# A hybrid attention / delta-net / PEER block: weights, U and V laid out anew, split weights kept in DRAM for the second half, and 448 gathered rows ahead of the dense pass

## The chip, the core and the metric

The kernel runs on one core of a Trainium2 chip. Its engines are TensorE (PE, matmuls into PSUM), VectorE (DVE), ScalarE (ACT), GpSimd (POOL) and SyncE (SP); 16 DMA engines move data between DRAM and the on-chip SBUF. SP issues the ordinary loads and stores of this kernel, POOL the indirect ones that gather rows by index. The metric is the device time of one execution in microseconds (us). The kernel before was run three times besides its profiled execution.

## The reference

One decoder block over 1024 tokens of width 1024, all float32: two token mixers in parallel, a gated merge, and a PEER feed-forward layer of 16,384 single-neuron experts. Cut to what matters here:

```python
h = rms_norm(x, mix_norm_w)
proj = h @ w_in            # 3x1024 stick-breaking q,k,v; 4x1024 delta net q,k,v,z; 16 b,a; 2x1024 gates
o_sb = stick_breaking_attention(q, k, v)                   # 8 heads of 128
o_gdn = gated_delta_rule_chunked(gq, gk, gv, g, beta)      # 8 heads of 128, then norm and silu(z)
merged = sigmoid(gate_sb) * (o_sb @ w_branch_sb) + sigmoid(gate_gdn) * (o_gdn @ w_branch_gdn)
x = x + merged @ w_out
h2 = rms_norm(x, ffn_norm_w)
q = h2 @ w_q                                               # 8 heads x 2 x 128
v1, i1 = top_k(q_1 @ keys1.T, 16); v2, i2 = top_k(q_2 @ keys2.T, 16)
vals, c = top_k(v1[..., :, None] + v2[..., None, :], 16)   # 16 of 256 pairs per head
expert = i1[c // 16] * 128 + i2[c % 16]; gate = softmax(vals)
# each token: 8 heads x 16 experts, with multiplicity
x = x + sum_over_experts(gate * gelu(h2 . peer_u[expert]) * peer_v[expert])
```

## The kernel before

**Numbers.** A float32 operand goes into TensorE as two rounded parts, hi and lo: `split` (L58) casts on ACT (L62) and subtracts on DVE (L63). `mm3` (L68) then makes three matmuls, hi·hi, hi·lo and lo·hi (L71 to L73).

**Stages.** The 1024 tokens are done in two halves of 512 (`half(0)`, `half(1)`). Each half runs stick-breaking attention (four pairs of heads), the gated delta net (four pairs), `gate_logits`, `merge`, `out_proj`, `ffn_norm` and `route`. Every weight comes through `load_w` (L87) in blocks of 256 columns: 12 for the attention, 16 for the delta net, 8 for the logits, 8 for the two branch matrices, 4 for `w_out` and 8 for `peer_w_q`, so 56 for each half, and one of 16 columns. A block is loaded on SP as two raw pieces of 512 KB (L93) and split in four pieces of 128x512; the pools `wp` and `wraw` hold two blocks and two raw pieces. The second half loads and splits the same weights again. A block serves 48 matmuls with 512 columns.

**The expert layer** is done in two ways. The token blocks 0, 1, 4 and 5 (128 tokens each) gather their rows: 128 experts a token, for U and for V, so 4 × 256 = 1024 indirect loads of 128 rows (512 KB, POOL, L1016), each followed by one DVE instruction over 128x1024 (L1019 for U, L1021 for V). The token blocks 2, 3, 6 and 7 go densely over all 128 blocks of 128 experts: `dense` (L856). For these, `gate_table` (L808) builds the full table of gates, 128 x 128 experts for each token, from one-hot matmuls, and stores it to DRAM (`g_d`, L854, 16 stores of 2 MB); `gates` loads it back, four expert blocks at a time (`d_g`, L906).

In the dense loop one expert block takes: `prep`, which loads 128 rows of U, transposes them with eight TensorE transposes (L877) into PSUM and splits them in two pieces; `scores`, 24 matmuls (L891, L893) and a Gelu (L895); `weigh`, the product with the gates (L922), the cast (L926) and the rest of the split (L913); `values`, which loads and splits rows of V; and 24 value matmuls into four PSUM accumulators (`pz1` and `pc`, two banks each), which are added to `d_acc` every eight blocks (L974). Scores run ahead of the weighing: seven are made inside the gate table's stage, spread over its four token blocks, and six weighings before the loop.

**Order.** A scheduler orders each engine's instructions by priority, in which `later(n)` puts work back. The gathered rows have the lowest priority, and each is tied behind an anchor: `gather(phase)` stands at the program's own steps and lets `PACE[phase]` rows go per step, behind the last DVE instruction issued there (L1028 to L1058). They begin with the second half; with the numbers of before, 353 of the 1024 rows stand ahead of the first weighing in DVE's order and the others in the dense loop. Four row buffers serve them, six within the dense loop. An engine executes its instructions in order, so a row whose data is late holds the DVE work behind it.

## Time and profile before

| | |
|---|---|
| runs | 3888.91, 3900.24, 3903.44 us; median 3900.24 |
| the profiled execution: time, span | 3908.46 us, 3906.7 us |
| busy: PE, DVE, ACT, POOL | 3674.3, 3089.5, 1753.0, 1298.8 us |
| moved by DMA | 939.72 MB, 241 GB/s over the span |
| the gathers' queue / the other loads and stores | 536.94 MB / 399.22 MB |
| mean granted PE clock | 0.971 |

The span is the profiled execution from its first to its last instruction. The profile gives each engine's busy time by source line and tile, what ended each wait, and how busy the 16 DMA engines were. The stages differ in what limits them, so the totals are read together with a table by stretch of the span. Line numbers are those of the kernel before.

### The profile page before, as it was taken

Reading aid. Unit: us, or ns where it says so; the run is one execution under the profiler, and the core shown is the slowest. Engines: PE = TensorE matmul, PEld = TensorE weight load, DVE = VectorE, ACT = ScalarE, POOL = GpSimd, SP = SyncE. Lnnn points to the kernel's source line nnn. Section 1 sums busy time; section 2 is a strip of 40 time slices with the busy share of each in tenths; the row PEclk is TensorE's granted clock in tenths of the full one; section 3 lists DMA queues with packets and bytes.
Section 4 is the critical chain, followed back from the end, with each engine's and each line's share of the span. In section 5 each row is a group of like instructions: output and inputs, shape, how many; then the busy total and the mean of one; then the engine's idle time right before and its main releaser. Section 6 shows DMA issues by size and latency. Waiting matters only on the chain. (4 is left out here: it accounts for less than half of the span.)

```text
span 3906.7 us, 55712 instructions
## 1 busy us (share of the span) xinstructions
PE 3674.3 (94%) x19976; PEld 3077.4 (79%) x19976; DVE 3089.5 (79%) x6330; ACT 1753.0 (45%) x3986; POOL 1298.8 (33%) x1034
## 2 busy tenths in 40 slices
PE   8999999999999999998877995899999999999997
PEld 7878888787777688886666884788888888888886
DVE  4345554349988988888789998899898899899898
ACT  6755555333777655543322994222222222222321
POOL 0000000000144322233341113655566555566555
PEclk9999999999999999999888998999999999999998
DMA  5221114552387766578884568899999999999998
GB/s 141 86 83 50 55 49 127 167 190 88 103 275 263 240 196 190 161 229 290 309 283 147 214 230 305 307 353 363 334 362 355 332 354 352 335 360 351 351 347 297
DMA packets 448230, 939.72 MB, mean 241 GB/s; under 512 B 44113, under 2 KB 239697, under 8 KB 445521
## 3 DMA queue, kind: packets, MB, share of 16 engines
q0 software_dynamic: 147456, 536.94, 39.1%
q1 hardware_dynamic: 300496, 399.22, 30.5%
q8 instruction: 157, 2.57, 0.3%
q14 instruction: 121, 0.98, 0.1%
HBM read 865.27 MB, written 70.25 MB: 239 GB/s over the span
## 5 line engine op out<-in xcount | busy, mean ns | idle before, releaser
L1016 POOL DMA_INDIRECT gb_row<-peer_u,expert x512 | 670.0, 1309 | 1879.1 <-DVE expert L796 1013.5
L1016 POOL DMA_INDIRECT gb_row<-peer_v,expert x512 | 627.6, 1226 | 714.9 <-DVE gb_h L1021 464.1
L1021 DVE SCALAR_TENSOR_TENSOR gb_h<-gb_row,gb_act,gb_h 128x1024 f32<-128x1024 f32 x512 | 656.1, 1281 | 60.6 <-DMA gb_row<-peer_v,expert 33.1
L1019 DVE SCALAR_TENSOR_TENSOR gb_row<-gb_row,gb_h 128x1024 f32<-128x1024 f32 x512 | 613.0, 1219 | 97.4 <-DMA gb_row<-peer_u,expert 77.6
L891 PE MATMUL mm<-hf,ut 128*128 128x512 f32 x2048 | 514.2, 398 | 0.0
L891 PEld LDWEIGHTS mm<-hf,ut 128*128 128x128 f32 x2048 | 376.1, 188 | 70.7
L63 DVE TENSOR_TENSOR w_lo<-w_raw,w_hi 128x512 fp32r<-128x512 f32 (+1 forms) x456 | 298.4, 676 | 166.7 <-ACT w_hi L62 128.5
L62 ACT CAST w_hi<-w_raw 128x512 fp32r<-128x512 f32 (+1 forms) x456 | 262.9, 615 | 275.6 <-PE mm L72 127.5
L71 PE MATMUL mm<-h,w_hi 128*128 128x512 f32 (+1 forms) x784 | 322.4, 411 | 4.0 <-ACT pj L587 4.0
L73 PE MATMUL mm<-h,w_lo 128*128 128x512 f32 (+1 forms) x784 | 319.9, 408 | 0.0
L72 PE MATMUL mm<-h,w_hi 128*128 128x512 f32 (+1 forms) x784 | 319.2, 407 | 0.0
L71 PE MATMUL mm<-w_hi,h 128*128 128x256 f32 x1024 | 301.3, 295 | 9.2 <-DVE x L636 4.7
L73 PE MATMUL mm<-w_hi,h 128*128 128x256 f32 x1024 | 294.6, 289 | 5.7 <-DVE h L63 5.7
L926 ACT CAST d_a<-u_act 128x512 fp32r<-128x512 f32 x128 | 79.4, 621 | 484.7 <-DVE u_act L922 483.9
L72 PE MATMUL mm<-w_lo,h 128*128 128x256 f32 x1024 | 296.0, 289 | 0.7 <-DVE w_lo L63 0.7
L893 PE MATMUL mm<-hf,ut 128*128 128x512 f32 x1024 | 260.3, 391 | 0.0
L895 ACT ACTIVATE u_act<-mm 128x512 f32<-128x512 f32 x128 | 77.0, 601 | 390.2 <-PE mm L893 376.5
L71 PE MATMUL pz<-d_v,d_a 128*128 128x512 f32 x512 | 201.6, 394 | 45.1 <-ACT d_a L926 30.8
L62 ACT CAST d_v<-v_raw 128x1024 fp32r<-128x1024 f32 x128 | 134.3, 1050 | 208.0 <-PE pc L73 175.9
L893 PEld LDWEIGHTS mm<-hf,ut 128*128 128x128 f32 x1024 | 192.3, 188 | 38.9
L71 PEld LDWEIGHTS mm<-w_hi,h 128*128 128x128 f32 x1024 | 200.6, 196 | 17.3 <-DVE x L636 5.2
L73 PEld LDWEIGHTS mm<-w_hi,h 128*128 128x128 f32 x1024 | 200.7, 196 | 7.8 <-DVE h L63 5.9
(332 smaller groups left out, 8632.4 us busy)
## 6 DMA issues: line engine op xcount, KB each, us to landing
w_raw<-w_in SPq DMA_DIRECT2D x144, 512.0 KB
u_raw<-peer_u SPq DMA_DIRECT2D x128, 512.0 KB
v_raw<-peer_v SPq DMA_DIRECT2D x128, 512.0 KB
g_d<-gt_stg SPq DMA_DIRECT2D x16, 2048.0 KB
d_g<-g_d SPq DMA_DIRECT2D x31, 1024.0 KB
w_raw<-peer_w_q SPq DMA_DIRECT2D x32, 512.0 KB
gl<-pj SPq DMA_DIRECT2D x32, 256.0 KB
th<-gl SPq DMA_DIRECT2D x32, 256.0 KB
```

The source lines that it names most:

```text
L62: nc.scalar.copy(hi, src)
L63: nc.vector.tensor_tensor(lo, src, hi.bitcast(F32), op=OP.subtract)
L71: mm(out, l[0], r[0], start=first, stop=False)
L72: mm(out, l[0], r[1], start=False, stop=False)
L73: mm(out, l[1], r[0], start=False, stop=last)
L891: mm(ps, ut[0][:, k], hx[a][:, k, x0:], start=k + a == 0, stop=False)
L893: mm(ps, ut[1][:, k], hx[0][:, k, x0:], start=False, stop=k == KD - 1)
L895: nc.scalar.activation(act, ps, AF.Gelu)
L926: nc.scalar.copy(hi, act)
L1016: nc.gpsimd.indirect_dma_start(out=r, out_offset=None, in_=self.i["peer_u" if p < n else "peer_v"][0], in_offset=bass.IndirectOffsetOnAxis ...
L1019: i = nc.vector.scalar_tensor_tensor(r, r, 1.0, h2, op0=OP.mult, op1=OP.mult, accum_out=act[:, q:q + 1])
L1021: i = nc.vector.scalar_tensor_tensor(acc, r, act[:, q:q + 1], acc, op0=OP.mult, op1=OP.add)
```

## The change

1. The host lays the inputs out anew before the launch: all projection weights as blocks of 256 columns, contiguous for each partition; the 16 columns of b and a apart (`w_ba`); the keys transposed (so `keys_T` with its 16 transposes goes); U transposed within each block of 128 experts (`u_t`); V by pairs of expert blocks and halves of the width (`v_t`). The raw copies of U and V stay for the gathers.
2. `load_w` keeps hi and lo of each block in DRAM when it is first used (two stores of 1 MB, in the first half). In the second half it loads hi and lo (two loads of 1 MB) straight into their places and splits nothing.
3. `prep` loads U already transposed into a pool of its own (two buffers) and splits it in one piece; its transposes go.
4. The gate table in DRAM has another order: a store of 2 MB now writes runs of 512 bytes, and a load reads 8 KB for each partition in one run (before 16 KB and 512 bytes).
5. Of the seven scores ahead, three are made within the gate table's stage and four behind its last matmul.
6. The four value accumulators rotate over six PSUM banks (`bank`).
7. `PACE` lets 448 rows go ahead of the dense pass and 4.5 a block within it.

```diff
-PACE = dict(sb=2.2, gdn=1.5, logits=2.5, merge=2.5, out=0.5, route=0, table=0.1, dense=5.25)
+PACE = dict(sb=2.4, gdn=2.4, logits=3, merge=2.5, out=0.5, route=0, table=0.1, dense=4.5)
...
-    def load_w(self, src, c0, n=CB):
-        hi = self.wp.tile([P, KD, n], F32R, name="w_hi")
-        lo = self.wp.tile([P, KD, n], F32R, name="w_lo")
+    def load_w(self, src, c0):
+        hi = self.wp.tile([P, KD, CB], F32R, name="w_hi")
+        lo = self.wp.tile([P, KD, CB], F32R, name="w_lo")
+        key = (src.tensor.name, c0)
+        if key in self.w_d:
+            for d, t in zip(self.w_d[key], (hi, lo)):
+                self.nc.sync.dma_start(t.bitcast(F32), d)
+            return hi, lo
         for k0 in range(0, KD, 4):
-            raw = self.wraw.tile([P, 4, n], F32, name="w_raw")
-            self.nc.sync.dma_start(raw, src[k0 * P:(k0 + 4) * P, c0:c0 + n].rearrange("(k p) n -> p k n", p=P))
+            raw = self.wraw.tile([P, 4, CB], F32, name="w_raw")
+            self.nc.sync.dma_start(raw, src[c0 // CB][:, k0:k0 + 4])
             for k in range(k0, k0 + 4, 2):
                 self.split(hi[:, k:k + 2], lo[:, k:k + 2], raw[:, k - k0:k - k0 + 2])
+        self.w_d[key] = [self.dr.tile([P, KD, CB], F32, name=f"wd{len(self.w_d)}_{a}") for a in range(2)]
+        for d, t in zip(self.w_d[key], (hi, lo)):
+            self.nc.sync.dma_start(d, t.bitcast(F32))
         return hi, lo
...
-                        mm(pg[:, u - u0], o2[:, u], o1[:, u], start=True, stop=True)
+                        self.last_gate = mm(pg[:, u - u0], o2[:, u], o1[:, u], start=True, stop=True)
...
-            nc.sync.dma_start(self.g_d[(n * P + c * GT) // GT], stg)
+            nc.sync.dma_start(self.g_d[:, :, (n * P + c * GT) // GT].rearrange("g p q t -> p g (q t)"),
+                              stg.rearrange("p (g q) t -> p g (q t)", q=GQ))
...
+            ur = pool(name="ur", bufs=2)
             def prep(e1):
-                raw = up.tile([P, D], F32, name="u_raw")
-                nc.sync.dma_start(raw, U[e1 * P:(e1 + 1) * P, :])
+                raw = ur.tile([P, KD, P], F32, name="u_raw")
+                nc.sync.dma_start(raw, U[e1])
                 ut = [up.tile([P, KD, P], F32R, name=f"ut{a}") for a in range(2)]
-                for k0 in range(0, KD, 4):
-                    ps = self.pz.tile([P, 4, P], F32, name="pz0")
-                    for k in range(4):
-                        nc.tensor.transpose(ps[:, k], raw[:, (k0 + k) * P:(k0 + k + 1) * P], self.ident)
-                    self.split(ut[0][:, k0:k0 + 4], ut[1][:, k0:k0 + 4], ps)
+                self.split(ut[0], ut[1], raw)
                 return ut
...
-                    nc.sync.dma_start(gts[-1][:, c:c + nc_],
-                                      self.g_d[c:c + nc_, :, e1:e1 + GQ, :].rearrange("c p q t -> p c q t"))
+                    nc.sync.dma_start(gts[-1][:, c:c + nc_], self.g_d[e1 // GQ][:, c:c + nc_])
...
+            def bank():
+                self.turn = (self.turn + 1) % 3
+                return (self.pc if self.turn == 2 else self.pz).tile([P, 512], F32, name=("pz0", "pz1", "pc")[self.turn])
...
-                nc.sync.dma_start(raw, V[e1 * P:(e1 + 2) * P, dh * 512:dh * 512 + 512].rearrange("(q p) d -> p q d", p=P))
+                nc.sync.dma_start(raw, V[e1 // 2, dh])
...
                     self.gate_table(n, blk, gt)
-                    for e1 in range(PRE * n // nb, PRE * (n + 1) // nb):
+                    if n < nb - 1:
+                        scores()
+                with self.tc.issue_after(self.last_gate.ins):
+                    while len(acts) < PRE:
                         scores()
...
                 if q == 0:
-                    ps = [self.pc.tile([P, 512], F32, name="pc") if n % 2 else self.pz.tile([P, 512], F32, name="pz1")
-                          for n in range(nb)]
+                    ps = [bank() for n in range(nb)]
...
-        b.g_d = dr.tile([len(b.dense_blks) * P // GT, P, P, GT], F32, name="g_d")
+        b.g_d = dr.tile([P // GQ, P, len(b.dense_blks) * P // GT, GQ, GT], F32, name="g_d")
```

Three places show how the instructions stand. The first is PE's order in the dense loop, from the end of one block's value matmuls to the next block's (`ut` holds the transposed U, `hf` the tokens, `d_v` V and `d_a` the weighted activations). Before:

```order
L73 MATMUL pc<-d_v_34405,d_a_34087 128x512
L877 MATMUL pz_34631<-ident,u_raw 128x128 x4
L877 MATMUL pz_34638<-ident,u_raw 128x128 x4
L891 MATMUL mm<-hf_19388,ut_34530 128x512
L891 MATMUL mm<-hf_19389,ut_34530 128x512
...
L893 MATMUL mm<-hf_19388,ut_34531 128x512 x8
L71 MATMUL pz_34701<-d_v_34500,d_a_34183 128x512
```

With the change (lines of the changed kernel):

```order
L74 MATMUL pz_32806<-d_v_32715,d_a_32615 128x512
L894 MATMUL mm<-hf_19369,ut_32833 128x512
L894 MATMUL mm<-hf_19370,ut_32833 128x512
...
L896 MATMUL mm<-hf_19369,ut_32834 128x512 x8
L72 MATMUL pz_32803<-d_v_32799,d_a_32694 128x512
```

The two groups of transposes between the value matmuls and the scores are gone; the other matmuls follow as before.

The second is PE's order at the end of the gate table (L838 and L851 are the table's matmuls, L844 and L857 in the changed kernel). Before:

```order
L838 MATMUL pz_22598<-gt_R,gt_L_20538 128x512
L851 MATMUL pc<-gt_o_22592,gt_o_22594 128x128 x8
L71 MATMUL pz_22931<-d_v_22877,d_a_22901 128x512
L72 MATMUL pz_22931<-d_v_22878,d_a_22901 128x512
L73 MATMUL pz_22931<-d_v_22877,d_a_22902 128x512
```

With the change:

```order
L844 MATMUL pz_22361<-gt_R,gt_L_20430 128x512
L857 MATMUL pc<-gt_o_22355,gt_o_22357 128x128 x8
L894 MATMUL mm<-hf_19369,ut_21847 128x512
...
L896 MATMUL mm<-hf_19369,ut_21848 128x512 x8
L894 MATMUL mm<-hf_19369,ut_22380 128x512
...
L896 MATMUL mm<-hf_19369,ut_22447 128x512 x8
L72 MATMUL pz_22736<-d_v_22682,d_a_22706 128x512
```

Four sets of 24 score matmuls now stand between the table's last matmul and the first value matmul, where the value matmuls followed directly.

The third is SP's order in the second half's merge (`th` are the stored logits, `o_raw` a mixer's output). Before:

```order
L93 DMA w_raw<-w_branch_gdn 128x4x256 x2
L608 DMA th<-gl_0_122 128x512
L608 DMA th<-gl_1_123 128x512
L93 DMA w_raw<-w_branch_gdn 128x4x256
L608 DMA th<-gl_2_124 128x512
L93 DMA w_raw<-w_branch_gdn 128x4x256
L608 DMA th<-gl_3_125 128x512
L601 DMA o_raw<-ogd_3_85 128x512
```

With the change:

```order
L97 DMA w_hi<-wd_0_7634 128x2048
L97 DMA w_lo<-wd_1_7635 128x2048
L628 DMA th<-gl_1_123 128x512
L628 DMA th<-gl_2_124 128x512
L97 DMA w_hi<-wd_0_7716 128x2048
L621 DMA o_raw<-ogd_3_85 128x512
L621 DMA o_raw<-ogd_4_86 128x512
L621 DMA o_raw<-ogd_5_87 128x512
L97 DMA w_lo<-wd_1_7717 128x2048
```

A block's two raw pieces of 512 KB become its hi and its lo part of 1 MB each, in the same queue among the logits and the mixers' outputs. Ahead of landmarks in DVE's order stand now these numbers of gathered rows (before in brackets): first merge product 303 (235), end of the merge 348 (268), end of the output projection 378 (293), first table operation 415 (323), first weighing 444 (353).

More of the change, by code (lines that the diff above doesn't have):

```diff
@@ L862, in dense @@
         NE1 = P
-        GQ = 4
         LEAD, SL, PRE, NA, AB, VB, GB = 6, 0, 7, 7, 10, 6, 2
-        U, V = self.i["peer_u"][0], self.i["peer_v"][0]
+        U, V = self.i["u_t"], self.i["v_t"]
         with ExitStack() as ctx:
@@ L1137, in block_kernel @@
                     b.consts(cp, cg, cm, tp)
-                with b.later(150):
-                    b.keys_T(tp)
             with ExitStack() as st:
```

71 lines of the change are left out of this document (37 added, 34 removed).

## The prediction

> **What bounds the kernel now.** I read the page's totals first, then a table of engine busy time by stretch of the program, then one expert block of the dense pass in order of time.
>
> ```profile
> span 3906.7 us, 55712 instructions
> PE 3674.3 (94%) x19976; PEld 3077.4 (79%) x19976; DVE 3089.5 (79%) x6330; ACT 1753.0 (45%) x3986; POOL 1298.8 (33%) x1034
> ```
>
> TensorE (PE) is busy 94% of the span, so a change pays where it takes work from PE, or where PE waits. The next rows say where that is. Their columns: stretch, its length, busy us (and instructions) of PE, PE weight load, DVE, ACT and POOL, granted PE clock, share of the DMA engines, GB/s.
>
> ```profile
> 0.00:655.00 655.00, 635.41 (x4158) 548.45 (x4159) 318.17 (x883) 400.38 (x1134) 1.17 (x10) 0.99 0.26 76
> 655.00:863.00 208.00, 197.93 (x1038) 166.54 (x1036) 94.22 (x162) 82.86 (x149) 0.00 (x0) 0.98 0.58 186
> 863.00:985.00 122.00, 114.00 (x566) 94.33 (x566) 105.56 (x573) 42.71 (x85) 0.00 (x0) 0.97 0.35 108
> 985.00:1330.00 345.00, 322.03 (x1780) 247.81 (x1780) 304.30 (x712) 268.61 (x725) 126.44 (x109) 0.96 0.67 218
> 1330.00:1761.00 431.00, 415.43 (x2619) 357.24 (x2618) 359.46 (x797) 227.80 (x578) 130.27 (x117) 0.98 0.64 202
> 1761.00:1930.00 169.00, 145.85 (x593) 114.66 (x591) 136.53 (x246) 64.22 (x111) 56.28 (x47) 0.93 0.87 295
> 1930.00:2012.00 82.00, 54.66 (x389) 52.58 (x390) 61.59 (x121) 18.26 (x40) 32.60 (x29) 0.80 0.90 312
> 2012.00:2142.00 130.00, 110.62 (x525) 88.67 (x523) 124.31 (x589) 33.47 (x61) 34.72 (x27) 0.93 0.56 181
> 2142.00:2372.00 230.00, 219.27 (x1462) 194.84 (x1462) 226.03 (x517) 210.21 (x487) 31.81 (x21) 0.97 0.59 218
> 2372.00:2500.00 128.00, 80.61 (x341) 64.90 (x341) 94.83 (x147) 31.18 (x44) 61.76 (x46) 0.82 0.91 317
> 2500.00:3830.00 1330.00, 1326.14 (x6285) 1104.67 (x6285) 1199.55 (x1534) 364.63 (x567) 781.07 (x596) 1.00 0.96 348
> 3830.00:3906.00 76.00, 52.34 (x234) 42.76 (x232) 64.99 (x59) 8.68 (x11) 42.63 (x36) 0.87 0.86 308
> 3400.00:3500.00 100.00, 100.00 (x475) 83.53 (x474) 93.61 (x151) 27.33 (x43) 62.29 (x46) 1.00 1.01 373
> ```
>
> The first three rows are the first half of the tokens; 985 to 2142 is the second half's attention, gated delta net, logits with merge, output projection and routing; 2142 to 2372 the gate table; then the handover and the dense loop. In the dense loop PE has no idle (1326 of 1330 us), so each PE instruction removed there is time, until DVE (1199.55, 90%) or the DMA engines (0.96) take its place. In the second half up to the table PE idles 23+16+23+27+19 = 108 us of 1157. In the handover and the start of the loop it idles 47 of 128 us.
>
> **The dense loop.** One block:
>
> ```profile
> 3796.69 1.03 PE L877 MATMUL pz<-ident,u_raw 128*128 128x128 f32 x8
> 3797.48 3.89 PE L891 MATMUL mm<-hf,ut 128*128 128x512 f32 x16
> 3801.20 1.98 PE L893 MATMUL mm<-hf,ut 128*128 128x512 f32 x8
> 3803.01 0.39 PE L71 MATMUL pz<-d_v,d_a 128*128 128x512 f32 x1
> 3808.23 0.39 PE L73 MATMUL pc<-d_v,d_a 128*128 128x512 f32 x1
> 3808.46 1.03 PE L877 MATMUL pz<-ident,u_raw 128*128 128x128 f32 x8
> ```
>
> The period is 3808.46 − 3796.69 = 11.77 us: 0.79 from the first transpose to the first score, 5.53 of scores, 5.45 of value matmuls. The U layout removes the eight transposes. The step from the transposes to the scores is 0.79 us; I add 0.07 for the two switches of kind around them, an estimate, so 0.86.
>
> ```profile
> L877 PE MATMUL pz<-ident,u_raw 128*128 128x128 f32 x1024 | 140.5, 275 | 11.5 <-DMA u_raw<-peer_u 9.8 <-DVE gt_er L821 0.8 <-DVE ut L63 0.8
> ```
>
> These 1024 transposes are 140.5 us of PE, an upper bound for all 128 blocks. The Trainium skill, TensorE: Matmul & The Clock Gate, Part 4: PE-mode transpose, puts a transpose in a kernel's context at about 275 ns, which is this row's mean; taken as time on PE, eight per block would be 2.2 us and 121 blocks 266 us, against the 104 that the steps in the block give. The trace speaks against that reading, since eight of them end 1.03 us after the first starts.
>
> The first seven blocks' transposes lie in the table stage, so 121 blocks × 0.86 = 104 us. Is the cover there, at 10.9 us a block?
>
> ```profile
> L1021 DVE SCALAR_TENSOR_TENSOR gb_h<-gb_row,gb_act,gb_h 128x1024 f32<-128x1024 f32 x342 | 438.3, 1281 | 21.1 <-DMA gb_h<-x2d 7.6 <-DMA gb_row<-peer_v,expert 7.2
> L1019 DVE SCALAR_TENSOR_TENSOR gb_row<-gb_row,gb_h 128x1024 f32<-128x1024 f32 x256 | 303.5, 1219 | 29.8 <-DMA gb_h<-h2d 14.6 <-DMA gb_row<-peer_u,expert 14.5
> L63 DVE TENSOR_TENSOR ut<-pz,ut 128x512 fp32r<-128x512 f32 x226 | 144.9, 682 | 1.6 <-ACT ut L62 1.6
> L63 DVE TENSOR_TENSOR d_v<-v_raw,d_v 128x1024 fp32r<-128x1024 f32 x113 | 139.5, 1234 | 2.0 <-ACT d_v L62 1.8
> ```
>
> DVE has 1199.55/113 = 10.6 us a block. The pace drops from 5.25 to 4.5 rows, 0.75 × 1.25 = −0.94; two splits of U (2 × 0.68) become one 1024 wide, priced as that of V (1.23), −0.13. That leaves 9.5 of 10.9 us, 88% where it was 90%. At the old pace it would be 10.5 of 10.9, so the fewer rows are what lets PE's gain through. DMA: U, V and the gates are 0.52 + 0.52 + 0.26 MB and a row 0.52, so 4.06 MB a block now and 3.67 after: 337 GB/s at 10.9 us, under the 348 measured, and V's and the gates' runs get longer. Both are close, and DVE's order also has waits, so I give back 5 us of the 104: **−99**. Bounds: −106 (nothing given back, 0.88 a block) and −40 (DVE or DMA holds the block at 11.4). The value banks go from four to six: at most the start of a group waits less, nothing at 1326 of 1330. In the last blocks, which score nothing, PE has 5.45 us of work but DVE the rows, 5.25 × 1.25 = 6.6; 0.75 row less for six blocks is **−5**, out of the tail's 24 idle us.
>
> **Gate table and handover.** The table stage of 230 us has ACT busy 210.
>
> ```profile
> L842 ACT ACTIVATE gt_o<-pz,gt_tr 128x128 f32<-128x128 f32 x256 | 95.1, 489 | 10.2 <-PE pz L838 10.2
> L852 ACT COPY gt_stg<-pc 128x512 f32<-128x512 f32 x127 | 78.9, 624 | 14.1 <-PE pc L851 12.8 <-issue 0.3
> L62 ACT CAST ut<-pz 128x512 fp32r<-128x512 f32 x20 | 13.0, 658 | 0.3 <-PE pz L877 0.3
> L895 ACT ACTIVATE u_act<-mm 128x512 f32<-128x512 f32 x7 | 4.5, 643 | 0.0
> ```
>
> Four of seven score sets move behind the last table matmul. With them go four Gelus (2.6 us) and most casts of U, for which 1024-wide ones come; I take **−7** for ACT. Also PE loses 4 × 5.53 + 7 × 0.8 = 28 us there, which does not end the stage, since ACT does. The 22 us of scores then stand in the handover:
>
> ```profile
> 2370.06 2.05 PE L851 MATMUL pc<-gt_o,gt_o 128*128 128x128 f32 x16 [0.94 <-ACT gt_o L845]
> 2402.90 0.80 PE L71 MATMUL pz<-d_v,d_a 128*128 128x512 f32 x1 [30.79 <-ACT d_a L926]
> 2372.76 0.32 SPq L854 DMA_DIRECT2D g_d<-gt_stg  x1
> 2383.33 3.16 SPq L906 DMA_DIRECT2D d_g<-g_d  x5
> 2401.51 1.89 DVE L922 TENSOR_TENSOR u_act<-u_act,d_g 128x512 f32<-128x512 f32 x3
> ```
>
> PE waits 30.79 us: the last store of the table (2.1 MB) takes until 2383.33, the gates are loaded behind it, and DVE comes to the first weighing (L922) only at 2401.51, behind rows and splits. The moved scores fill this gap and do not shorten it. What shortens it is DVE's order: some 11 rows and 5 splits ahead of that product, 11 × 1.25 + 5 × 1.2 ≈ 20 us, so the wait ends after about 24 us: **−7**. The new store writes 512-byte runs, so it can be later; the load reads 8 KB runs. With PE busy in the gap the clock, 0.82 in this stretch, should fall less: **−2**. Sum −16; bounds 0 (the chain store, load, product unchanged and the table no shorter) and −35 (the whole wait gone).
>
> **The second half.** It splits no weights:
>
> ```profile
> L1019 DVE SCALAR_TENSOR_TENSOR gb_row<-gb_row,gb_h 128x1024 f32<-128x1024 f32 x195 | 236.5, 1220 | 58.4 <-DMA gb_row<-peer_u,expert 57.4
> L1021 DVE SCALAR_TENSOR_TENSOR gb_h<-gb_row,gb_act,gb_h 128x1024 f32<-128x1024 f32 x128 | 163.8, 1280 | 21.8 <-DMA gb_row<-peer_v,expert 21.2
> L63 DVE TENSOR_TENSOR w_lo<-w_raw,w_hi 128x512 fp32r<-128x512 f32 (+1 forms) x220 | 143.3, 674 | 9.3 <-ACT w_hi L62 9.2
> L62 ACT CAST w_hi<-w_raw 128x512 fp32r<-128x512 f32 (+1 forms) x220 | 126.9, 615 | 142.4 <-PE mm L72 36.8 <-PE mm L73 33.6 <-DMA w_raw<-peer_w_q 30.1
> ```
>
> DVE loses 143 us and ACT 127; DVE gets back some 91 rows (the order has 444 ahead of the first weighing where 353 were), 91 × 1.25 = 114 us. So DVE gains 29 net, in the wrong places for a large gain: of PE's 108 idle us I let a third go, **−35** (attention 12, delta net 8, routing 15, where no rows were put).
>
> Against that stands DMA. Each of 56 weight blocks is 2.1 MB instead of 1.05, and in longer runs. In attention and delta net the shares 0.67 and 0.64 leave room: 28 blocks and 43 rows add 52 MB, some 144 us at 362 GB/s (348 at share 0.96), and 269 are free. From 1761 to 2142 they do not: there 99 MB moved in 381 us (295 × 169 + 312 × 82 + 181 × 130), and 24 blocks (25 MB) and 49 rows (26 MB) come on top: 150 MB, 414 us at 362 GB/s. That is +33 where all of it must be done in place; some rows can slip into the table stage (share 0.59), so **+29**. Bounds: 0, where it slips, and +61 at the 339 GB/s of this stretch (295 at 0.87). A row that is late holds DVE in order, with the merge products and the splits of the mixers' outputs behind it, and PE waits for those.
>
> A second cost is the slot: a block can be loaded only when its place is free, with no raw copy ahead of it. The cover is the other slot's block, 48 matmuls × 5.45/24 = 10.9 us of PE; at 362 GB/s 2.1 MB take 5.8 us. I take nothing, and price it among the rivals. Net of the second half: **−6**.
>
> **The first half** stores both parts of each block, 117 MB on SP's queue. Its DMA shares (0.26, 0.58, 0.35) hold that: at 362 GB/s 324 us, against 653 free ones. SP issues a store behind the last split of a block, and the next raw load behind the store, so a raw load starts later, by less than the 10.9 us of PE's block. The merge is fullest (0.58, 20 blocks): **+6**, an estimate of 0.3 us a block; and **−3** for the keys, whose 16 transposes (0.1 us each by the step above), copies and loads go. Bounds −3 and +40 (2 us for each of 20 blocks).
>
> **Sum** on the profiled execution, 3908.46 (span 3906.7): −99 −5 −16 −6 +3 = −123, so 3785. The three runs shown lie at 3888.91 to 3903.44 with median 3900.24, 8 us under the profiled one, so the forecast for the runs is **3778**.
>
> **Rivals.**
> A: the second half becomes a DMA stage. For it: 0.87 and 0.90 already in merge and projection, PE idle 50 of 251 us there. Against: 373 GB/s at a share of 1.01 in 3400 to 3500, so there is room with long runs. Relief lost (35) and the upper DMA bound (+32 more): +67, **3845**. The Trainium skill, DMA: Bandwidth & Descriptors, Specifications, gives about 358 GB/s per core; by it 150 MB would take 419 us, 5 more than by 362, and the 373 of the trace is above it.
> B: the relief comes and the merge costs nothing (rows slip): −29 and −25 more of PE's 108 idle us: **3724**.
> C, the other side: each second-half block arrives late because its load waits for the slot. For it: gathers take 0.52 MB pieces of the same engines, and the 2.1 MB store above needed up to 10.6 us (2372.76 to 2383.33), the whole cover. Against: attention and delta net put other PE work between blocks. It decides from 123/56 = 2.2 us a block, a load of 13.1 us, 160 GB/s; at 3 us late, +168: **3946**.
> D: the dense loop ends at DVE's pace, 11.4 us a block, since waits between DVE's instructions (10% now) grow: 0.5 × 121 = +60, **3838**.
>
> **How the numbers follow.** Forecast 0.63, A 0.14, B 0.13, C 0.05, D 0.05. The range 3715 to 3850 takes in A, B and D and leaves out C and the far ends of A and B; the forecast's own is 3750 to 3805. About 0.5% (20 us) is what a measurement can tell from no change: slower takes C (0.05), faster all that ends under 3880, 0.91, and 0.04 stay for mixtures between A, D and C that end near 3900.
>
> **What will show it.** The dense block's period from first score to first score: 10.9 to 11.0; over 11.3 is D. In the same stretch no L877, DVE near 88%, PE still without idle. Value matmuls begin about 24 us after the last table matmul with 22 of them in scores. From the merge to routing a DMA share over 0.95 and a stretch of about 385 to 400 us; over 430 is A, under 365 B. PE's waits for w_hi and w_lo loads: a few single us; over 2 us on most blocks is C. First half within 10 us of 985. I am wrong if the loop keeps its 11.77, or if the second half gives back over 100 us.

## The result

The changed kernel takes 3947.69 us (median of 4 runs, 3942.28 to 3948.20) against 3898.45 before (4 runs, 3888.91 to 3903.44): the ratio is 1.0133, 95% interval 1.0112 to 1.0153. It is slower by 1.3%, where 3778 was forecast, and lies outside the range of 3715 to 3850.

First the totals of the changed kernel's profiled execution:

```profile
span 3945.4 us, 53165 instructions
PE 3595.3 (91%) x18936; PEld 2995.3 (76%) x18936; DVE 2956.2 (75%) x5972; ACT 1655.6 (42%) x3623; POOL 1330.7 (34%) x1034
```

PE is busy 79 us less, DVE 133 and ACT 97, and the span is 38.7 us longer. To see where it went, both spans are divided at the same four events: the end of the first half's routing, the end of the second half's routing (in each, the last instruction of its top-16 search over the keys), the first value matmul and the last one. The columns are those of the stretches in the prediction. Before:

```profile
0.00:979.00 979.00, 941.83 (x5734) 803.82 (x5734) 511.94 (x1602) 525.13 (x1362) 1.17 (x10) 0.99 0.34 103
979.00:2142.60 1163.60, 1054.08 (x5924) 866.45 (x5924) 992.80 (x2480) 613.17 (x1515) 380.32 (x327) 0.95 0.69 225
2142.60:2402.90 260.30, 219.38 (x1462) 194.84 (x1462) 251.02 (x553) 213.35 (x492) 47.70 (x33) 0.92 0.64 233
2402.90:3882.40 1479.50, 1458.98 (x6856) 1212.33 (x6856) 1317.31 (x1685) 401.35 (x618) 861.87 (x659) 0.99 0.96 344
```

With the change:

```profile
0.00:996.10 996.10, 945.44 (x5706) 805.84 (x5706) 506.94 (x1592) 520.21 (x1347) 1.17 (x10) 0.98 0.61 220
996.10:2295.40 1299.30, 1080.19 (x5946) 889.62 (x5946) 978.32 (x2413) 509.39 (x1301) 483.22 (x419) 0.91 0.79 283
2295.40:2564.20 268.80, 211.77 (x1308) 176.59 (x1308) 247.33 (x506) 211.70 (x476) 46.51 (x31) 0.97 0.71 212
2564.20:3922.80 1358.60, 1357.81 (x5976) 1123.29 (x5976) 1208.49 (x1452) 414.27 (x500) 793.15 (x569) 1.00 0.93 341
```

| stretch | before | after | difference | forecast |
|---|---|---|---|---|
| first half | 979.0 | 996.1 | +17.1 | +3 |
| second half to the end of routing | 1163.6 | 1299.3 | +135.7 | −6 |
| gate table and handover | 260.3 | 268.8 | +8.5 | −16 |
| value matmuls, first to last | 1479.5 | 1358.6 | −120.9 | −99 |
| what follows | 24.3 | 22.6 | −1.7 | −5 |

The dense pass gave more than was forecast. The second half took all of it back, and more. There PE idles 219 us where it idled 110, and is busy 26 us longer for nearly the same matmuls, at a granted clock of 0.91 instead of 0.95.

**The dense loop** does what the prediction said. One block of the changed kernel: its scores, the last of its value matmuls and the next block's first scores:

```profile
3699.65 3.79 PE L894 MATMUL mm<-hf,ut 128*128 128x512 f32 x16
3703.28 1.98 PE L896 MATMUL mm<-hf,ut 128*128 128x512 f32 x8
...
3710.30 0.39 PE L74 MATMUL pz<-d_v,d_a 128*128 128x512 f32 x1
3710.53 0.84 PE L894 MATMUL mm<-hf,ut 128*128 128x512 f32 x3
```

The period is 10.88 us (11.77 before), with no transposes; PE is busy 1357.8 of the stretch's 1358.6 us and DVE 89%.

**The second half.** The waits of DVE, before and after (us in total, times, longest):

```profile
DVE gb_row L1019 <- DMA gb_row<-peer_u,expert: 57.4, 36, 4.7
DVE gb_h L1021 <- DMA gb_row<-peer_v,expert: 21.2, 20, 2.6
```

```profile
DVE gb_row L1028 <- DMA gb_row<-peer_u,expert: 180.1, 101, 7.3
DVE gb_h L1030 <- DMA gb_row<-peer_v,expert: 39.8, 21, 5.0
```

DVE waits 220 us for gathered rows that have not landed, where it waited 79. What stands behind such a row in DVE's order stands still with it, and PE too where it needs that work. PE's own longest waits in that stretch of the changed kernel:

```profile
PE pz L315 <- ACT sb_hi L63: 26.2, 6, 8.5
PE mm L72 <- DVE part L633: 17.2, 4, 7.9
PE pz L592 <- ACT g_dec L589: 17.0, 4, 6.9
PE mm L72 <- ACT o L63: 14.4, 3, 11.0
PE pz L505 <- DVE g_nrm L486: 14.3, 2, 11.7
...
PE mm L72 <- DMA w_hi<-wd: 10.5, 2, 6.7
```

They belong to the attention, the merge, the delta net and others: many different steps, none over 12.4 us. Followed back in the trace from each wait of PE to what released it, step by step, 143 of PE's 219 idle us lead to a gathered row; before, 50 of 107 did. PE's waits for the weights themselves are a small part, 20.5 us.

The growth lies in two stages. Divided at the last update of the delta net's state, the second half is attention and delta net (first row), then logits to routing (second row). Before:

```profile
979.00:1760.70 781.70, 742.66 (x4420) 610.30 (x4421) 669.46 (x1523) 497.21 (x1305) 256.71 (x225) 0.97 0.65 208
1760.70:2142.60 381.90, 311.42 (x1506) 256.15 (x1504) 323.34 (x958) 115.96 (x210) 123.61 (x102) 0.90 0.77 260
```

With the change:

```profile
996.10:1828.30 832.20, 746.54 (x4408) 617.76 (x4409) 646.34 (x1442) 435.19 (x1173) 304.42 (x267) 0.95 0.74 258
1828.30:2295.40 467.10, 333.65 (x1540) 271.86 (x1538) 331.98 (x973) 74.20 (x128) 178.80 (x152) 0.85 0.88 328
```

The first grew by 50 us and the second by 85. In the second the DMA engines are nearly full up to the end of the merge (share 0.95 and 362 GB/s from 1828 to 2067) and less so behind it.

**The handover.** Lines around the end of the table in the changed kernel, from PE, SP's queue and DVE:

```profile
2529.26 2.05 PE L857 MATMUL pc<-gt_o,gt_o 128*128 128x128 f32 x16 [0.94 <-ACT gt_o L851]
2551.14 1.98 PE L896 MATMUL mm<-hf,ut 128*128 128x512 f32 x8
2564.25 0.79 PE L72 MATMUL pz<-d_v,d_a 128*128 128x512 f32 x1 [11.13 <-ACT d_a L928]
2531.96 0.36 SPq L860 DMA_DIRECT2D g_d<-gt_stg  x1
2553.85 1.91 SPq L909 DMA_DIRECT2D d_g<-g_d  x4
2560.78 2.50 DVE L924 TENSOR_TENSOR u_act<-u_act,d_g 128x512 f32<-128x512 f32 x4 [5.67 <-DMA d_g<-g_d]
```

The last store of the table takes 21.9 us (2531.96 to 2553.85) where it took 10.6. The first value matmul comes 33 us after the last table matmul's end, 31 before; the four sets of scores fill 22 of these. The rest of the 8.5 us is the table itself, which takes 236 us up to its last matmul instead of 230.

### The profile page after: what moved, and what is told of

Same layout as the page of the kernel before. It is cut to its first block, busy times and chain, and to the rows that moved or that the text cites. A ratio compares the mean times of both kernels' runs of the same rounds, so it can differ in the third digit from the quotient of the medians.

```text
span 3945.4 us, 53165 instructions
## 1 busy us (share of the span) xinstructions
PE 3595.3 (91%) x18936; PEld 2995.3 (76%) x18936; DVE 2956.2 (75%) x5972; ACT 1655.6 (42%) x3623; POOL 1330.7 (34%) x1034
## 4 chain that ended last, share of the span: by engine, by line
PE 66%; DMA 9%; issue 9%; DVE 7%; POOL 5%; ACT 4%; SPq 0%; POOLq 0%; DVEq 0%; ACTq 0%
PE mm L894 10%; PE mm L72 6%; PE mm L74 6%; PE mm L73 6%; PE mm L896 5%; POOL gb_row L1025 5%; DMA gb_row<-peer_u,expert 4%; PE pz L74 3%; PE pz L72 3%; PE pz L73 3%; PE pc L857 3%; DMA gb_row<-peer_v,expert 2%; PE pz L541 2%; PE pz L535 2%; PE pc L74 2%
## 5 line engine op out<-in xcount | busy, mean ns | idle before, releaser
L1025 POOL DMA_INDIRECT gb_row<-peer_v,expert x512 | 658.9, 1287 | 910.1 <-DVE gb_h L1030 675.2
L894 PE MATMUL mm<-hf,ut 128*128 128x512 f32 x2048 | 490.4, 391 | 10.7 <-ACT ut L63 9.7
L894 PEld LDWEIGHTS mm<-hf,ut 128*128 128x128 f32 x2048 | 385.6, 188 | 91.1 <-ACT ut L63 9.9
L72 PE MATMUL mm<-w_hi,h 128*128 128x256 f32 x1024 | 304.4, 298 | 22.8 <-DVE x L656 9.0
L74 PE MATMUL mm<-w_hi,h 128*128 128x256 f32 x1024 | 300.9, 295 | 13.3 <-DVE h L64 13.1
L64 DVE TENSOR_TENSOR w_lo<-w_raw,w_hi 128x512 fp32r<-128x512 f32 (+1 forms) x226 | 148.7, 682 | 181.4 <-ACT w_hi L63 150.1
L72 PE MATMUL pz<-d_v,d_a 128*128 128x512 f32 x680 | 265.6, 391 | 11.1 <-ACT d_a L928 11.1
L74 PE MATMUL pz<-d_v,d_a 128*128 128x512 f32 x680 | 265.4, 390 | 0.7 <-DVE d_a L915 0.7
L73 PE MATMUL pz<-d_v,d_a 128*128 128x512 f32 x680 | 265.3, 390 | 0.0
L63 ACT CAST ut<-u_raw 128x1024 fp32r<-128x1024 f32 x128 | 135.1, 1056 | 304.7 <-PE mm L894 288.7
L896 PE MATMUL mm<-hf,ut 128*128 128x512 f32 x1024 | 256.3, 391 | 0.0
L72 PEld LDWEIGHTS mm<-w_hi,h 128*128 128x128 f32 x1024 | 205.1, 201 | 30.5 <-DVE x L656 9.8
L896 PEld LDWEIGHTS mm<-hf,ut 128*128 128x128 f32 x1024 | 192.7, 188 | 39.6
L74 PEld LDWEIGHTS mm<-w_hi,h 128*128 128x128 f32 x1024 | 204.5, 200 | 17.8 <-DVE h L64 13.9
```

Source lines behind the costliest of these rows:

```text
L63: nc.scalar.copy(hi, src)
L64: nc.vector.tensor_tensor(lo, src, hi.bitcast(F32), op=OP.subtract)
L72: mm(out, l[0], r[0], start=first, stop=False)
L73: mm(out, l[0], r[1], start=False, stop=False)
L74: mm(out, l[1], r[0], start=False, stop=last)
L894: mm(ps, ut[0][:, k], hx[a][:, k, x0:], start=k + a == 0, stop=False)
```

## The experiments

Two questions had to be settled: why the second half grew, and what the parts are worth. All times of a stretch are between the same events as above. "Kept" means that the second half loads kept split weights, "split twice" that it splits the raw weights again. The rows are those that DVE executed by the end of routing. Times of a stretch come from one execution of each kernel. They repeat well: the kernel before and four variants that split twice with the same 323 rows took 1162.4 to 1168.7 us for the second half, and the first half took 975.3 to 980.4 us in eight kernels that keep nothing and 994.1 to 996.6 in five that keep the weights in 8 KB runs.

**1. The two parts of the change, undone singly and together.**

```diff
-PACE = dict(sb=2.4, gdn=2.4, logits=3, merge=2.5, out=0.5, route=0, table=0.1, dense=4.5)
+PACE = dict(sb=2.2, gdn=1.5, logits=2.5, merge=2.5, out=0.5, route=0, table=0.1, dense=5.25)
```

> The changed kernel with the numbers of PACE from before (353 rows ahead, 5.25 a block in the dense loop). In the changed kernel the second half up to the table took 1293 us where it took 1157, and DVE waited 180 us there for U rows. Theory 'weights': the 2.1 MB loads of split weights make the rows late; then with fewer rows the stretch falls only by about 30 us and the whole is about 3940. Theory 'rows': the 91 more rows are too many for the stretch whatever the weights do; then some 110 us go, dense gives back 25 (5.25 rows), and the whole is about 3860. Theory 'slot': PE waits for weights that may only be loaded when a place is free; then nothing changes in the second half, 3970.

```diff
-        self.w_d[key] = [self.dr.tile([P, KD, CB], F32, name=f"wd{len(self.w_d)}_{a}") for a in range(2)]
-        for d, t in zip(self.w_d[key], (hi, lo)):
-            self.nc.sync.dma_start(d, t.bitcast(F32))
```

> The changed kernel without the store of split weights: the second half loads and splits the raw blocks again, as before, from the new layout; 448 rows ahead. Theory 'weights': the second half falls by some 110 us and the first by 17, about 3820. Theory 'rows': DVE has 143 us of splits and 114 us of rows more than before in a stretch where it was 85% busy, so the second half stays near 1270, first half -17: about 3905. Theory 'slot': the wait goes with the raw copies ahead of the slots, second half about 1160, 3800.

Both edits together:

> Both undone: no split weights in DRAM and the numbers of PACE from before; U and V, the gate table, the score places and the banks as changed. All three theories: the second half returns to about 1157 us, less a little for longer runs; the first half to 985. What it tells apart is the dense loop: at 5.25 rows a block DVE has 10.5 us of work for 10.9 us of PE. If DVE then bounds it the period is about 11.2 to 11.4 us and the whole about 3835; if not, 10.9 and about 3800.

Measured: numbers of before with kept weights 3945.38 us (1.0122, 1.0105 to 1.0139); split twice with the new numbers 3922.49 (1.0074, 1.0047 to 1.0100); both undone 3877.05 (0.9940, 0.9918 to 0.9961). The stretches, second half and then value matmuls, of the three in this order:

```profile
994.30:2234.00 1239.70, 1078.12 (x5941) 888.46 (x5942) 900.95 (x2310) 507.21 (x1298) 397.72 (x352) 0.93 0.75 268
2492.90:3928.10 1435.20, 1382.54 (x5977) 1134.17 (x5975) 1308.73 (x1571) 390.76 (x504) 927.73 (x657) 0.98 0.95 354
```

```profile
976.80:2145.50 1168.70, 1055.71 (x5934) 867.71 (x5934) 992.72 (x2477) 614.09 (x1513) 383.01 (x327) 0.95 0.68 225
2420.20:3898.50 1478.30, 1396.84 (x5976) 1145.05 (x5976) 1310.92 (x1574) 393.69 (x503) 911.86 (x660) 0.96 0.93 346
```

```profile
979.60:2146.80 1167.20, 1055.94 (x5934) 867.90 (x5934) 993.38 (x2476) 613.64 (x1513) 381.21 (x327) 0.96 0.68 225
2418.10:3858.20 1440.10, 1387.35 (x5976) 1137.14 (x5976) 1310.42 (x1574) 392.35 (x503) 920.70 (x659) 0.98 0.95 355
```

What follows. Keeping the weights makes the second half 72 us longer at the old numbers (1239.7 against 1167.2), and the first half 15 (994.3 against 979.6); the new numbers add 60 to the second half (1299.3) and take 77 from the dense pass (1435.2 to 1358.6). None of the three theories was met by all three runs. The "weights" theory had 3940 for the first and was near, but 3820 for the second, which came out at 3922. The third was to take 3800 or, with DVE as the bound, 3835, and took 3877. The reason is one that no theory had: with splits in the second half the new numbers are not obeyed. The scheduler gives rows the lowest priority, and with DVE full it placed 323 by the end of routing, the same as with the old numbers, and 353 ahead of the first value matmul with either set. The 95 rows left over went into the dense pass on top of the 4.5 a block and made it longer (1478.3, PE idle 81 us) than with 5.25 (1440.1). So with splits it is not a larger PACE that brings more rows ahead in these stages: DVE's room bounds them, and the kept weights made that room.

The third run also tells what the removed transposes are worth at the old number of rows: the value matmuls take 1440.1 us where they took 1479.5, 39 less. The other 82 us of the changed kernel's dense pass come with the 89 to 91 rows fewer in it.

**2. Without rows.** PACE with 3 rows ahead and 8 a block in the dense pass (which says nothing here), once with kept weights, once split twice; each ran once (4321.52 and 4290.63 us in all):

```diff
+PACE = dict(sb=0.05, gdn=0, logits=0, merge=0, out=0, route=0, table=0, dense=8)
```

> The changed kernel with 3 rows ahead and 8 a block in the dense loop; only the second half is looked at (dense then goes by DVE, about 14 us a block). Theory 'slot': the second half up to the table stays over 1200 us and PE's waits for w_hi and w_lo stay at 20 us or grow. Theories 'weights' and 'rows': it falls under 1100 us, since no row is held up and holds DVE up, and PE's 108 idle us of before mostly go.

> The control for the run with 3 rows ahead: the same, but the second half splits its weights again and nothing is kept in DRAM. Only the second half is looked at. With split weights loaded it took 1066 us to the end of routing (996.6 to 2063.0). If the splits cost the second half time of their own, as the prediction had it (a third of PE's idle time, 35 us), this one takes about 1100. If PE's waits come from the rows alone, it takes 1066 again, and keeping split weights is worth nothing even without rows.

The second half of the one and of the other:

```profile
996.60:2063.00 1066.40, 1025.01 (x5939) 846.58 (x5940) 514.19 (x1747) 497.79 (x1291) 6.76 (x7) 0.98 0.38 140
```

```profile
976.50:2029.50 1053.00, 1024.02 (x5928) 844.94 (x5929) 640.20 (x1964) 602.46 (x1507) 8.53 (x7) 0.99 0.28 89
```

Without rows PE idles 41 us with kept weights and 29 with splits. So taking away the splits, 126 us of DVE and 105 of ACT, gains the second half nothing in all; PE's idle time beyond these 29 us comes with the rows. By stage, attention and delta net take 7 us less without the splits (712.2 for 719.5), and logits to routing 21 more (354.1 for 333.4): keeping weights costs 13 us in the sum. PE's longest wait in the kept kernel's stretch is for a weight, and its waits for weights make 17 us:

```profile
PE mm L72 <- DMA w_hi<-wd: 14.4, 3, 10.0
```

**3. What makes the rows late with kept weights: run length, bytes, buffers or order?** The same bytes in runs of 1 KB instead of 8 KB:

```diff
-                self.nc.sync.dma_start(t.bitcast(F32), d)
+                self.nc.sync.dma_start(t.bitcast(F32), d.rearrange("k p n -> p k n"))
...
-        self.w_d[key] = [self.dr.tile([P, KD, CB], F32, name=f"wd{len(self.w_d)}_{a}") for a in range(2)]
+        self.w_d[key] = [self.dr.tile([KD, P, CB], F32, name=f"wd{len(self.w_d)}_{a}") for a in range(2)]
         for d, t in zip(self.w_d[key], (hi, lo)):
-            self.nc.sync.dma_start(d, t.bitcast(F32))
+            self.nc.sync.dma_start(d.rearrange("k p n -> p k n"), t.bitcast(F32))
```

> The changed kernel with the split weights in DRAM laid out so that each run is 1 KB instead of 8 KB; the instructions' order is the same. Theory 'long runs crowd the rows out': a row's 4 KB runs get turns more often between 1 KB runs than between 8 KB ones, as they did before the change; the second half falls by 50 or more and the whole is about 3890. Theory 'amount': what counts is how long the DMA engines are busy, and short runs take longer for the same bytes; then the second half grows and the whole is about 3990.

3939.15 us (1.0100, 1.0083 to 1.0117); second half 1288.7. By their times both theories fell: 10 us less, neither 50 less nor more. The waits say more. DVE's wait for rows fell from 220 to 176 us, so rows did come earlier between short runs; and PE's waits for the weights rose from 20.5 to 65 us:

```profile
PE mm L74 <- DMA w_lo<-wd: 40.3, 10, 6.9
PE mm L72 <- DMA w_hi<-wd: 24.9, 6, 10.4
```

Run length moved the lateness from the rows to the weights, and the sum hardly changed.

One row buffer more:

```diff
-        self.row_bufs = [(self.gp, f"gb_row{k}") for k in range(4)]
+        self.row_bufs = [(self.gp, f"gb_row{k}") for k in range(4)] + [(self.gpx, "gb_row6")]
...
-            b.wraw = right("wraw", 2)
+            b.wraw = right("wraw", 1)
+            b.gpx = right("gpx", 1)
```

> The changed kernel with five row buffers instead of four in the second half (one raw weight buffer instead of two pays for it, which can cost the first half some us); the scheduler puts 447 rows ahead. DVE idled 243 us before rows in the second half, where it had idled 80. Theory 'depth': rows come late since only four can be under way; with five the idle time falls to some 150 and the second half by 50 or more. Theory 'supply': the DMA engines and POOL deliver rows no faster while weights are loaded; the idle time stays over 220 and the whole at 3940 to 3960.

4260.37 us (1.0912, 1.0892 to 1.0933), which tells of the price paid for the buffer: with a single raw buffer the first half took 1257.5 us instead of 996, PE waiting there 108 us for hi parts of weights, and from the end of routing to the first value matmul it took 370 us instead of 269. The second half alone took 1262.5, 37 less than with four buffers, DVE's wait for rows 193 us instead of 220. "Depth" had expected 50 or more and a wait of some 150, "supply" a wait over 220: some of the lateness is depth, most is not.

Half the bytes (the lo part of the first block stands in for all, so that the second half's weights are less exact):

```diff
-            for d, t in zip(self.w_d[key], (hi, lo)):
-                self.nc.sync.dma_start(t.bitcast(F32), d)
-            return hi, lo
+            self.nc.sync.dma_start(hi.bitcast(F32), self.w_d[key][0])
+            if self.one_lo is None:
+                self.one_lo = self.wp.tile([P, KD, CB], F32R, name="w_lo")
+                self.nc.sync.dma_start(self.one_lo.bitcast(F32), self.w_d[key][1])
+            return hi, self.one_lo
```

> The changed kernel, but the second half loads only the hi part of each block; one lo part, that of its first block, stands in for all (so the second half's weights are less exact: their rounding rest is another block's). The second half moves 59 MB less, nothing is split, and the scheduler puts as many rows ahead (415 at the table, where it puts 415). Theory 'bytes': DVE's idle time before rows (243 us) and the second half (1299 us to the end of routing) grew because the weights' transfers keep the rows late; with half of them gone it falls to 1200 or less, the whole to 3850. Theory 'order': rows are late since DVE's order has them with less work of its own between them; then the second half stays within 30 us of 1299.

3879.38 us (0.9958, 0.9945 to 0.9970). The second half, with the same 415 rows:

```profile
995.70:2227.20 1231.50, 1063.17 (x5946) 876.97 (x5946) 975.04 (x2413) 510.30 (x1301) 485.26 (x419) 0.93 0.73 253
```

68 us less: between the two expectations, so bytes are a part and not the whole. Then the bytes alone, added to the kernel that splits twice at the old numbers. A first variant copied 1 MB from DRAM to DRAM with each block:

> Split twice with the numbers of PACE from before (second half 1167 us, whole 3877), and in the second half each weight block also starts a copy of 1 MB from DRAM to DRAM that nobody reads: the traffic of the split weights without the change of DVE's order. Theory 'bytes': the rows come late as in the changed kernel; the second half grows by 50 or more. Theory 'order': 53 of the 59 MB go through free DMA time (shares 0.56 to 0.67 outside merge and projection), and the second half grows by less than 20.

It says nothing on the question: 3880.12 us (0.9955, 0.9941 to 0.9969), but nothing holds such a copy back, and the scheduler put them into the first 300 us (DMA share there 0.85 instead of 0.32), where they cost nothing either (the first half took 980.4 us). The second variant stores each block's hi part behind its split:

```diff
+        if key in self.w_d:
+            junk = self.dr.tile([P, KD, CB], F32, name=f"junk{c0}_{src.tensor.name}")
+            self.nc.sync.dma_start(junk, hi.bitcast(F32))
+        self.w_d[key] = True
```

> Split twice with the numbers of PACE from before, and in the second half each block's hi part is stored to a place in DRAM that nobody reads, in 8 KB runs behind its split: 59 MB more traffic in the second half, DVE's order as without it (318 rows ahead of the table, where 323 stood). It replaces the copies from DRAM to DRAM, which ran in the first 300 us instead of the second half, so that their run says nothing. Theory 'bytes': the second half grows from 1167 us by 50 or more. Theory 'order': by less than 20.

3911.70 us (1.0025, 1.0014 to 1.0035), where the same kernel without the stores had 0.9940; the second half:

```profile
975.30:2165.80 1190.50, 1061.67 (x5934) 869.72 (x5934) 988.58 (x2467) 616.12 (x1515) 375.37 (x322) 0.95 0.76 266
```

+23 us, between the two expectations again; DVE's wait for rows is 112 instead of 85. Then the order: kept weights, with PACE numbers (sb 1.6, gdn 1.45, logits 0.8, merge 2.1, out 1.6) that keep the scheduler from bringing rows forward into DVE's new room:

> The changed kernel with numbers of PACE chosen so that the rows stand in DVE's order about as before the change (91 by the end of the attention, 235 at the first merge product, 290 at the routing; before 100, 235, 307) while split weights are loaded; 5.75 rows a block in the dense loop, which is not looked at. The second half took 1240 us with 348 rows bunched ahead by the scheduler and 1167 with 323 rows and no kept weights. Theory 'order': with the rows spread as before it takes 1150 to 1170. Theory 'bytes': it stays at 1210 or more.

```profile
994.10:2195.40 1201.30, 1065.65 (x5940) 878.35 (x5941) 831.81 (x2194) 503.85 (x1296) 327.66 (x294) 0.93 0.69 251
```

1201 us with 290 rows (one run, 3998.24 us in all), again between: 38 us less than with 348 rows, and 34 more than the kernel that splits twice and has 323. So neither theory is the whole. The stages tell them apart, divided as in the result (rows executed in each in brackets):

| kernel | attention and delta net | logits to routing |
|---|---|---|
| split twice, no rows | 719.5 (3) | 333.4 (0) |
| kept, no rows | 712.2 (3) | 354.1 (0) |
| split twice, old numbers | 788.3 (221) | 378.9 (102) |
| kept, few rows | 780.8 (213) | 420.5 (77) |
| kept, old numbers | 815.9 (253) | 423.7 (95) |
| kept, half the bytes | 808.2 (270) | 423.3 (145) |
| kept, new numbers (the change) | 832.2 (264) | 467.1 (151) |

- Attention and delta net: with nearly as many rows, keeping the weights costs nothing (712.2 for 719.5, 780.8 for 788.3). The change's 51 rows over those 213 go with 51 us, and half the bytes takes 24 of them away.
- Logits to routing: here the kept weights cost by themselves, 21 us without a row and 42 with 77 rows, which are fewer than the 102 of the kernel that splits. In this run PE waits 37 us for weights. The 56 rows between 95 and 151 go with another 43 us, and half the bytes takes 44 away.

The parts do not add: 59 MB of stores more cost 23 us with 318 rows, and 59 MB of loads less gained 68 with 415. How much of the rows' price is their place in the order and how much their number was not separated.

**4. The rows without kept weights, and a better kernel.** Split twice at the old numbers, with the gate table in DRAM in its old order:

```diff
-            nc.sync.dma_start(self.g_d[:, :, (n * P + c * GT) // GT].rearrange("g p q t -> p g (q t)"),
-                              stg.rearrange("p (g q) t -> p g (q t)", q=GQ))
+            nc.sync.dma_start(self.g_d[(n * P + c * GT) // GT], stg)
...
-                    nc.sync.dma_start(gts[-1][:, c:c + nc_], self.g_d[e1 // GQ][:, c:c + nc_])
+                    nc.sync.dma_start(gts[-1][:, c:c + nc_],
+                                      self.g_d[c:c + nc_, :, e1:e1 + GQ, :].rearrange("c p q t -> p c q t"))
```

> Split twice with the numbers of PACE from before (3877 us), and the gate table in DRAM in its old order: stores of 16 KB runs, loads of 512-byte runs. In the changed kernel the last store of the table took 21.9 us where it had taken 10.6, and the first value matmul waits for it. If that is the handover's cost, the time from the end of routing to the first value matmul falls by 11 us from 271, and the whole is about 3866. If the loads' 512-byte runs cost the dense loop (DMA at 0.95) more than that, the loop grows from 1440 to 1455 or more and the whole is 3880 or above.

3870.34 us (0.9925, 0.9907 to 0.9944): the fastest of all, 0.75% under the kernel before. Against the new order (0.9940) the intervals overlap, so the order of the table is worth at most a few us either way. The last store fell from 19.7 to 15.4 us, and the time from the end of routing to the first value matmul stayed (271.9 for 271.3); the value matmuls took 1431.4 us, where the second expectation had them grow to 1455. The time came near the 3866 of the first expectation, but not for its reason, so that is chance.

The same with the new numbers enforced by a higher priority of the rows:

```diff
-        with self.later(1000000):
+        with self.later(300):
```

> Split twice, the gate table in its old order, and the rows' priority raised so that the numbers of PACE of the change are kept (441 rows by the end of routing, where 323 stood), 4.5 a block in the dense loop. From 3 to 323 rows the second half grew by 114 us, 0.36 us a row; if a row goes on costing that, 118 more cost 42 and the dense loop gives back 73 (1431 to 1358): about 3840. If rows cost what they did with split weights loaded (0.56 and more), with DVE also busy with splits, they cost 100 or more and the whole is about 3900.

4031.38 us (1.0351, 1.0318 to 1.0383), far over both expectations. Second half and value matmuls:

```profile
978.00:2391.50 1413.50, 1130.45 (x5925) 914.72 (x5926) 1139.31 (x2657) 617.38 (x1514) 521.22 (x445) 0.87 0.69 230
2652.80:4008.90 1356.10, 1355.33 (x5977) 1121.25 (x5975) 1202.54 (x1447) 412.11 (x499) 799.84 (x566) 1.00 0.95 339
```

The dense pass reaches the same 1356 us, so it needs fewer rows left in it and not the kept weights. But 118 rows more, forced ahead with the splits still there, cost the second half 246 us (1413.5 against 1167.2).

**The price of a row.** Rows by the end of routing and time of the second half (the rows' places differ too, most in the forced run):

| | rows | us | us per further row |
|---|---|---|---|
| split twice | 3 | 1053.0 | |
| split twice | 323 | 1167.2 | 0.36 |
| split twice, forced | 441 | 1413.5 | 2.1 |
| kept | 3 | 1066.4 | |
| kept, few rows | 290 | 1201.3 | 0.47 |
| kept, old numbers | 348 | 1239.7 | 0.66 |
| kept, new numbers | 415 | 1299.3 | 0.89 |

In the dense pass a row fewer saves 0.86 us (1435.2 − 1358.6 over the 89 rows between 355 and 444 executed ahead of the first value matmul). With kept weights the rows beyond 348 cost some 0.9, where rows beyond 323 forced in among splits cost 2.1; how they would cost with the same priority in both was not tested. But 0.9 is no less than the row saves, the kept weights raise the price of the rows before these, and they cost 15 to 20 us in the first half.

## Why the prediction failed, step by step

- **Dense loop, −99 and −5: right in its mechanism, short in its sum.** The period is 10.88 us (10.9 forecast), 0.89 less than before, where 0.86 was taken (0.79 read and 0.07 estimated); DVE is 89% busy (88), PE without idle. PE's busy time fell by 101 us, where 104 were forecast. The measured −120.9 still lies past the bound of −106: it holds 20 idle us at the start of the loop (1479.5 − 1459.0 before, 1 after), which the sum left out. Most of them were waits for the additions to `d_acc`, and the six banks alone did not take them away: with six banks and 353 rows ahead PE waits 47 us for them, where it had waited 19 with four, and with 444 rows ahead not at all. That fewer rows are what lets PE's gain through was right: without that, 39 us came. The tail gave 1.7 of its 5. PE's waits with six banks and 353 rows ahead (split twice, old numbers):

```profile
PE pz L72 <- DVE d_acc L980: 30.9, 13, 4.7
PE pc L72 <- DVE d_acc L980: 16.1, 6, 4.7
```

- **Second half, −6: the step that failed**, +135.7. Each of its terms was wrong:
  - "Of PE's 108 idle us I let a third go, −35": as far as the runs show, this idle time came with the rows and not with the splits. Without rows the splitting kernel idles 29 us in all, and keeping the weights takes nothing away in the sum. Fifteen of the 35 were put on the routing, "where no rows were put"; but 30 rows stood there before and 37 with the change, as the landmarks ahead of the prediction say. From the end of the output projection to the end of routing it took 146.6 us before and 127.3 and 129.3 without rows, with and without kept weights.
  - The 91 rows (92 by the end of routing) were set against DVE's busy time alone, and since DVE came out 29 us ahead, PE was charged nothing. Attention and delta net, forecast at −20, grew by 50 us with 43 rows more.
  - The DMA term, +29 for the stretch from 1761 to 2142, measured +85 (381.9 to 467.1 us) and is past its upper bound of 61 too. Its bytes were right, 153 MB for 150. Its rate was not: it took the engines at 362 GB/s without a pause, and they moved 328 at a share of 0.88.
  - "I take nothing" for the slot: PE waits 17 us for kept weights without rows, 20.5 with the change and 37 with 290 rows.
- **The sign it had named came:** the second half gave back over 100 us.
- **What the sum should have noted in the profile of before:** the waits of DVE for rows, 79 us in this stretch, next to PE's 108 idle us. DVE was 85% busy there, and its longest waits stood in front of rows; in front of weight splits it waited 9 us.
- **Gate table and handover, −16: wrong**, +8.5 (table +6, handover +2). "Which does not end the stage, since ACT does" did not hold: with the scores moved out the table took 236 to 242 us in the changed kernel and in every variant with two raw buffers, where it had taken 230. It is not DVE either, though DVE was busy 226 of 230 us: without rows DVE is busy 205 us and the table takes 240 (split twice):

```profile
2029.50:2269.40 239.90, 193.08 (x1220) 161.15 (x1220) 205.19 (x467) 202.13 (x463) 1.88 (x2) 0.99 0.53 152
PE pc L854 <- ACT gt_o L848: 24.0, 26, 0.9
...
ACT gt_stg L855 <- PE pc L854: 26.9, 50, 1.2
```

PE and ACT wait for each other there, in many short waits (PE for ACT 5 us before, 39 with the change). That the moved scores had filled PE's waits was not tested.

In the handover, rows were again what counted, and not the store's 512-byte runs. With the old numbers and kept weights no row stands between the table and the first value matmul; the same store takes 9.3 us, and the value matmuls follow 21.6 us behind the table, right behind the scores:

```profile
2471.96 0.36 SPq L860 DMA_DIRECT2D g_d<-gt_stg  x1
2481.24 1.28 SPq L909 DMA_DIRECT2D d_g<-g_d  x3
2491.11 1.98 PE L896 MATMUL mm<-hf,ut 128*128 128x512 f32 x8
2492.92 0.39 PE L72 MATMUL pz<-d_v,d_a 128*128 128x512 f32 x1
```

All six variants without a row there take 21.6 us; those with 7 or 8 rows take 31 to 34.

- **First half, +3: inside its bounds** of −3 to +40, +17.1, but past the 10 us that its sign allowed. With the copies left out it is 15 us shorter (979.6). The time is lost in logits, merge and projection (+17.6 together), the fullest stage of that half, as was said.
- **The rivals.** The time, 3948, is almost rival C's (3946), and that is chance: C had every block late, and PE waited about 20 us for late weights in seven waits. Rival A had the place of the larger part: from logits to routing the stretch took 467 us, past the 430 that was its sign. It priced that stage at +61, where it grew by 85, and had no growth in attention and delta net. What happened, rows late under more traffic and more rows, holding DVE and through it PE from the attention to the routing, was stated as a sentence behind the DMA term ("A row that is late holds DVE in order") and never made a rival with a price.
- **The new numbers of PACE** were taken as the cause of the 444 rows ahead. At the rows' low priority they are only an upper bound: with splits the scheduler stays at 323 by the routing with either set, and only a higher priority brought 441.

## What to carry to other kernels

Work that is filled into another stage must be priced at the engine that bounds the stage, at the margin: not by whether the filling engine has idle time, but by what waits behind it in order when its data is late. A run without the filler, with and without the change, shows at once whose the idle time is. Before taking work off an engine that is 85% busy, look at what its remaining idle time stands in front of: here DVE's wait for rows grew from 79 to 220 us when the splits were gone and more rows came. And price added transfers at the rate and share that a stage of this kind has shown, with its pauses (here 328 GB/s at 0.88), not at the best stretch of the trace.

## What the runs showed of the hardware beyond that

- The granted clock of PE was lower where PE stalled more: 0.99 in the second half without rows and with splits (29 idle us), 0.95 before (110), 0.91 with the change (219) and 0.87 with rows forced ahead (283). PE's busy time for nearly the same matmuls went from 1024 to 1054, 1080 and 1130 us. Of the 136 us lost, 26 are PE being busy longer.
- 59 MB of copies from DRAM to DRAM in the first 300 us, at a DMA share of 0.85, cost nothing that can be measured; 59 MB of stores spread over the second half, where rows are gathered, cost 23 us there.
- The same split weights in runs of 1 KB instead of 8 KB made 10 us difference in the second half (1288.7 and 1299.3), but moved the waits: DVE's for gathered rows from 220 to 176 us, PE's for the weights from 20.5 to 65.
- A store of 2 MB in 512-byte runs took 9.3 us with no row gathers beside it and 21.9 with them.
- Taking eight 128x128 transposes, 275 ns each in the profile, out of a block shortened it by 0.89 us, 0.11 us each (11.77 to 10.88).
- The second raw weight buffer is worth 260 us in the first half of this kernel.
